# A pair's statistics through ScalarE's queue, the halves of attention's outputs copied and added by VectorE behind the near maximum, and four edits at the ends of the later stages

## The chip, the core and the metric

The kernel is one program on one core of a Trainium2 chip. The metric is the device time of one execution in microseconds (us), the median of several runs. A core has five engines that each take their instructions in order: TensorE (PE), VectorE (DVE), ScalarE (ACT), GpSimd (POOL) and SyncE (SP). They wait for each other by semaphores. DMAs are issued here by SP, POOL and ACT, and an engine that waits for a semaphore holds up whatever stands behind it in its queue, DMA issues among it.

## The reference

One layer of a decoder over 2048 tokens of width 1024, all in float32:

```python
hn = _rmsnorm(h, ln_mix[i])
z = hn @ w_in[i]
...
att = _dilated_attention(q, k, v, slopes).reshape(B, S, ATT_WIDTH)
pool = _multiscale_pool(u, pool_w[i], pool_scale[i])
h = h + jnp.concatenate([att, pool], axis=-1) @ w_out[i]
hn = _rmsnorm(h, ln_ffn[i])
up = _causal_dwconv(hn @ w_up[i], conv_w[i], conv_b[i])
gate, val = jnp.split(up, 2, axis=-1)
h = h + (jax.nn.silu(gate) * val) @ w_down[i]
g = jax.nn.sigmoid(_rmsnorm(h, ln_ple[i]) @ w_ple_gate[i])
h = h + g * (p[i] @ w_ple[i])
...
return _rmsnorm(h, ln_final)
```

The attention has 8 heads of 64 and three branches, with windows of 128, 512 and 2048 tokens and dilations of 1, 4 and 16; only the causal keys within the window count. Each branch gives an output, a row maximum and a softmax denominator, and the branches are mixed with weights denominator x exp(maximum - largest maximum).

## The kernel before

**Stages.** By the profile's time: the input projection and the pooling groups to 403 us, attention to about 738, the output projection with its norms to 905, the up products with convolution and gate (44 turns) to 1805, the down products to 2281, and the per-layer-embedding gate with the final norm, in five pieces of tokens (three of 512, two of 256), to the end. Nearly every float32 product is made of three matmuls on values that are split into a high part (made by ACT) and a low part (what is left, made by DVE or POOL): `split`, L83, and `mm3`, L88.

**Attention** (`phase_attention`). Heads go in pairs. A pair has 32 steps, 16 blocks of 128 queries for each head, and the kernel has 128 steps in all. In a step PE makes near scores (L572, L573) and far scores (L561, L562), DVE adds the biases and takes the row maxima (near L577, far L583), ACT makes the exponentials with their sums (near L589, far L593), PE turns them over (L600), ACT copies the high half (L613), DVE makes the low half (L617), and PE multiplies with the values (L628 far, L642 near). The order on all engines is written by hand: the list `ord` in `CFG` names the stages with a lag in steps, and every step runs down that list.

```python
'ord': [['B', 0], ['M', 0], ['N', 0], ['S', 1], ['o', 7], ['F', 0], ['h', 2], ['nm', 0], ['fm', 0], ['l', 2], ['T', 1], ['V', 6], ['W', 6], ['ne', 0], ['fe', 0]]
```

N and F are the scores, nm and fm the maxima, ne and fe the exponentials, T the turn, h and l the halves, V and W the values, o the fold, S the statistics, M the mixing.

**The fold.** Four query blocks make a group, with one output of 128 x 512 for the far branches and one for the near branch. The upper and lower 64 partitions of the output are the products with the high and low halves of the values, so they are added: `halves_sum` lets ACT copy one half to SBUF (L657) and DVE add the other (L658). That occurs at every second step, 64 times. The output's pool in PSUM has one buffer, so the next V on PE waits for that add.

**The pair's statistics.** At the end of each of the first three pairs, `mix_stats` has PE transpose maxima and denominators (L754, L757), DVE copy them to SBUF (sx L759, sy L761), and POOL's queue store them to memory (std L763, stf L764) and load them in another layout (sn L767, sf L771). With d counted in steps from the next pair's start, `mix_lift` (L845 to L850, DVE and ACT) works on them at d = 9 and `mix_weights` (to L863) at d = 10; from d = 13 POOL fetches the weights (wb, L874), multiplies (L884 to L891) and stores the results (L907, L908) in four rounds, four steps apart, which reach into the next pair.

**Later places.** In `phase_rest` the last turn of the up products writes yg (L1495) to memory from SP's queue (L1496); the down products read it as ra (L1542, also SP) and split it. Before the last stage the gate's weights (wg) and the embedding's (w_ple, raw tile rwp) are loaded and split. `close` makes a piece's result, and `add_square` sums its squares (L155). A list `tk` holds what is due after so many ticks; a tick is a group of gate and embedding matmuls. `one` makes the final norm's sums on PE (st, L100) and its inverse root.

Of the kernel before, what the change touches and what calls it, by code (L numbers as in the profile page):

```python
# [13 lines left out]
ALU = mybir.AluOpType  # L14
# [5 lines left out]
KD = D // P  # L20
S = 2048
# [19 lines left out]
V_N = V_CB + 2 * NF  # L41


CFG = {"tt": 2, "ee": 2, 'ord': [['B', 0], ['M', 0], ['N', 0], ['S', 1], ['o', 7], ['F', 0], ['h', 2], ['nm', 0], ['fm', 0], ['l', 2], ['T', 1], ['V', 6], ['W', 6], ['ne', 0], ['fe', 0]], 'perm': [3, 2, 1, 0], 'fp': [[0], [1], [2], [3]], 'np': [[0, -1], [1], [2], [3]], 'm': [9, 10, 13, 4, 6, 7]}


class Shared:
# [438 lines left out]
def phase_attention(tc, g, mx, near_b, far_b):  # L486
# [5 lines left out]
    with ExitStack() as ctx:  # L492
# [145 lines left out]
        def far_pv(gi, kbs, first):  # L638
            gr = groups[gi]
            for kb in kbs:  # L640
                for pt in (gr.h, gr.l):
# [7 lines left out]
                    )  # L649
                    first = False  # L650

        def halves_sum(dst, o, e):

            mine = slice(DH * e, DH * e + DH)
            other = slice(DH * (1 - e), DH * (1 - e) + DH)
            ev = sb.tile([P, CH], F32, tag="ev", bufs=2, name="ev")
            nc.scalar.copy(ev[mine], o[other])  # L657
            nc.vector.tensor_tensor(dst, o[mine], ev[mine], op=ALU.add)  # L658

        def values(v):  # L660
            gi, part = v // 4, v % 4
# [15 lines left out]
        def fold(v):  # L677
# [9 lines left out]
            else:  # L687
                halves_sum(pt.s1[mine, q * CH : (q + 1) * CH], gr.o, e)
                groups.pop(gi)

        def stats(s):
            if (s + 1) % (2 * NQ) == 0:
                pr = s // (2 * NQ)
                if pr < NPAIR - 1:
                    mix_stats(nc, g, mx, ps_t, pr, pairs[pr])
                else:
                    last_near(nc, g, mx, ps_t, pairs[pr])

        def mix(s):
            for pr in range(NPAIR - 1):  # L700
                d = s - (pr + 1) * 2 * NQ
                if d == CFG["m"][0]:
                    mix_lift(nc, g, mx, pairs[pr])
                if d == CFG["m"][1]:
                    mix_weights(nc, g, mx, pr, pairs[pr])
                for c in range(NCH):
                    if d == CFG["m"][2] + CFG["m"][3] * c:
                        mix_fetch(nc, g, mx, nc.gpsimd, pr, pairs[pr], c)
                    if d == CFG["m"][2] + CFG["m"][3] * c + CFG["m"][4]:
                        mix_products(nc, g, mx, nc.gpsimd, pairs[pr], c)  # L710
                    if d == CFG["m"][2] + CFG["m"][3] * c + CFG["m"][5]:
                        mix_store(nc, g, mx, nc.gpsimd, nc.gpsimd, pr, pairs[pr], c)()
# [5 lines left out]
        with tc.manual_schedule(engines=set(EN.values())):  # L718
            for dst, src in load_qk(0):
                rdma(nc, dst, src)  # L720
            for q in range(4):
                for which in ("v3", "v1"):
                    rdma(nc, *load_v(0, which, q))
            queue = []
            stages = {
                "F": far_scores, "N": near_scores, "fm": far_max, "nm": near_max, "fe": far_exp, "ne": near_exp,
                "T": turn, "h": high, "l": low, "V": values, "W": values_b, "S": stats, "M": mix, "o": fold, "B": begin
            }
            for s in range(NS + 10):
                if s < NS:  # L730
                    h, n = divmod(s, NQ)
                    if n == 1 and h + 1 < H:
                        queue += load_qk(h + 1)
                    if queue:
                        rdma(nc, *queue.pop(0))
                    for pr in range(1, NPAIR):
                        if s - 2 * NQ * (pr - 1) in V_STEPS:
                            rdma(nc, *load_v(pr, *V_STEPS[s - 2 * NQ * (pr - 1)]))
                if s == NS + 2:
                    last_far(nc, g, mx, ps_t, pairs[NPAIR - 1])  # L740
                    pieces = pairs[NPAIR - 1].pieces = last_weights(nc, mx, pairs[NPAIR - 1])
                for nm, lag in CFG["ord"]:
                    if 0 <= s - lag < NS or nm == "M":
                        stages[nm](s - lag)
                for _ in range({NS + 3: 3, NS + 4: 2, NS + 5: 1}.get(s, 0)):
                    next(pieces)
# [4 lines left out]
def mix_stats(nc, g, sb, psum, pr, pt):  # L751

    tp = psum.tile([P, 1024], F32, tag="t", name="tps")
    nc.tensor.transpose(tp[:64, :P], pt.st1.rearrange("p a e n -> p (a e n)"), g.ident)  # L754
    far = tp[:16, CH:].rearrange("p (c r) -> p r c", r=4)
    for r in range(4):
        nc.tensor.transpose(far[:, r, :], pt.st3[:, r].rearrange("p a e i -> p (a e i)"), g.ident)  # L757
    sx = sb.tile([64, P], F32, tag="sx", name="sx")
    nc.vector.tensor_copy(sx, tp[:64, :P])  # L759
    sy = sb.tile([16, CH], F32, tag="sy", name="sy")  # L760
    nc.vector.tensor_copy(sy, tp[:16, CH:])  # L761
    q = nc.gpsimd
    q.dma_start(g.std[pr], sx)  # L763
    q.dma_start(g.stf[pr], sy)  # L764
    pt.sn = sb.tile([P, 2, 2, 16], F32, tag="sn", name="sn")
    pt.sf = sb.tile([P, 2, 2, 16], F32, tag="sf", name="sf")
    q.dma_start(  # L767
        pt.sn.rearrange("p a e r -> p (a e) r"),
        g.std[pr].rearrange("(ae n) q -> ae (n q)", n=NQ).rearrange("ae (i r) -> i ae r", r=16),
    )  # L770
    q.dma_start(  # L771
        pt.sf.rearrange("p a e r -> p (a e) r"),
        g.stf[pr].rearrange("(ae n) q -> ae (n q)", n=4).rearrange("ae (i r) -> i ae r", r=16),
    )
# [138 lines left out]
def phase_rest(tc, g, mxs, mx, last_pair, xT, pT, w_out, w_up, w_down, w_gate, w_ple, outT):  # L913
# [3 lines left out]
    with ExitStack() as ctx:  # L917
# [463 lines left out]
        with tc.manual_schedule(engines=set(EN.values())):  # L1381
# [8 lines left out]
            for i in range(len(turns) + 1):  # L1390
# [102 lines left out]
                    add(cur.uv[:, hi_], cur.c)  # L1493
                if prev:
                    nc.vector.tensor_tensor(prev.yg, prev.yg, prev.yv, op=ALU.mult)  # L1495
                    nc.sync.dma_start(g.act[prev.f][:, prev.half * 1024 : prev.half * 1024 + 1024], prev.yg)  # L1496
                splits(6)
                sum_t4(i + 2)
                after(6)
# [118 lines left out]
        aux[0] = db  # L1618
        ahead(len(order))
        wg = [units.pop(("g", 0, k)) for k in range(NW)]  # L1620
        wg += [load_w2(db, rows(w_gate, k), f"wg{k}", nc.vector if k % 2 else None) for k in range(NW, KD)]
        wp = []
        for k in range(KP):
            raw = sb.tile([P, 1024], F32, tag="raw", bufs=2, name="rwp")
            nc.sync.dma_start(raw, rows(w_ple, k))
            hi = db.tile([P, 1024], F32R, tag="wph", bufs=2, name="wph")
            lo = db.tile([P, 1024], F32R, tag="wpl", bufs=2, name="wpl")
            split(nc, hi, lo, raw, nc.vector if k % 2 else None)
            wp.append((hi, lo))

        HF = CH // 2
# [17 lines left out]
        for i, (t0, n, off, row) in enumerate(pieces):  # L1649
# [23 lines left out]
            def close(j, gp, pl):  # L1673
# [10 lines left out]
                if last and j == KD - 1:  # L1684
                    sq = db.tile([P, CH], F32, tag="nt", bufs=3, name="sq")[:, :n]
                    nc.scalar.activation(sq, ht, AF.Square)
                    sqs.append(sq)
                else:
                    add_square(nc, db, acc, ht, j == 0)

            if i == 0:
                for grp in range(2):
# [43 lines left out]
                for j in range(KD):  # L1736
                    tk.later(j // 2, lambda j=j: scaled(j))

            tk.later(1, one)
        tk.flush()  # L1740


# [127 lines left out]
```

## Time and profile before

| what | us |
|---|---|
| median of 3 runs | 2526.32 (2522.40 to 2528.23) |
| the profiled execution | 2537.44 |
| its span | 2535.3 |
| busy PE, DVE, ACT, POOL | 2417.9, 1579.9, 1106.6, 527.8 |
| attention, 403 to 738: PE, DVE, ACT, POOL busy | 273.8, 245.7, 257.2, 115.5 |
| mean granted clock: whole span, attention | 0.978, 0.93 |

The page sums each engine's busy time over the span; PE is the fullest by far, but attention, with PE busy 273.8 of 335 us, is its loosest long stage. In the views, `out<-in` names tiles, a bracket at the end of a timeline row gives the idle time before an instruction and what ended it, and "PEclk" or "granted clock" is 1.00 at full speed.

### The profile page before, as it was taken

The numbers are of one execution on the slowest core, as the hardware profiler recorded it, in microseconds if no ns is written. First come the engines' busy times: TensorE is split into PE (matmuls) and PEld (weight loads), VectorE is DVE, ScalarE is ACT, GpSimd is POOL, SyncE is SP. The second block draws the span as 40 slices with busy tenths as digits, with TensorE's granted clock in tenths as the row PEclk, the third lists the DMA queues.
The fourth block names the chain that finished last, engine by engine and source line by source line (L and its number), as shares of the span: only waits on it lengthen the run. The fifth ranks groups of instructions, "written<-read, shape, count | busy, mean of one in ns | idle before, by whom it ended". The sixth has DMA issues, their size and how long they took to land.

```text
span 2535.3 us, 31890 instructions
## 1 busy us (share of the span) xinstructions
PE 2417.9 (95%) x11515; PEld 2026.2 (80%) x11515; DVE 1579.9 (62%) x2414; ACT 1106.6 (44%) x1923; POOL 527.8 (21%) x436
## 2 busy tenths in 40 slices
PE   8999998887779999999999999999999999999998
PEld 7888887776667877888887888888788888887788
DVE  6645427876664467888888666666435464444664
ACT  5423326887641135444446444444323243323332
POOL 3312221054420023343340000000122222212000
PEclk9999999998889999999999999999999999999999
DMA  7534358696646774445556333333646474644332
GB/s 238 170 123 179 141 176 252 168 202 169 159 161 224 220 241 168 166 173 184 174 196 207 121 121 133 121 120 109 199 134 218 142 239 143 198 145 143 121 104 88
DMA packets 205933, 424.10 MB, mean 167 GB/s; under 512 B 39392, under 2 KB 65632, under 8 KB 202704
## 3 DMA queue, kind: packets, MB, share of 16 engines
q1 hardware_dynamic: 170720, 368.94, 46.1%
q0 software_dynamic: 18912, 25.75, 3.1%
q10 hardware_dynamic: 16144, 27.38, 2.9%
q8 instruction: 91, 1.49, 0.3%
q14 instruction: 66, 0.54, 0.1%
HBM read 290.01 MB, written 131.89 MB: 166 GB/s over the span
## 4 chain that ended last, share of the span: by engine, by line
PE 74%; DMA 8%; issue 7%; DVE 4%; ACT 2%; POOL 2%; SPq 0%; POOLq 0%; DVEq 0%; ACTq 0%
PE ua L1298 18%; PE uc L1298 9%; PE dn L89 6%; PE dn L90 6%; PE dn L91 6%; PE ub L1298 4%; PE z L91 4%; PE z L89 4%; PE z L90 4%; DMA wb<-wd 3%; PE o L91 2%; PE o L89 2%; PE o L90 2%; PE gp L89 2%; PE gp L90 2%
## 5 line engine op out<-in xcount | busy, mean ns | idle before, releaser
L89 PE MATMUL dn<-ah,hd 128*128 128x512 f32 x704 | 275.4, 391 | 4.5 <-ACT ah L84 4.5
L90 PE MATMUL dn<-al,hd 128*128 128x512 f32 x704 | 275.0, 391 | 0.1
L91 PE MATMUL dn<-ah,ld 128*128 128x512 f32 x704 | 274.7, 390 | 0.0
L85 POOL TENSOR_TENSOR ld<-rd,hd 128x1024 fp32r<-128x1024 f32 x42 | 100.9, 2403 | 814.9 <-DVE yg L1318 466.3
L84 ACT CAST hd<-rd 128x1024 fp32r<-128x1024 f32 x88 | 92.6, 1052 | 265.9 <-PE dn L90 230.4
L85 DVE TENSOR_TENSOR al<-ra,ah 128x512 fp32r<-128x512 f32 x88 | 116.4, 1325 | 136.3 <-ACT ah L84 136.3
L89 PE MATMUL z<-hnh,wh 128*128 128x512 f32 (+1 forms) x480 | 171.2, 357 | 9.1 <-ACT hnh L252 5.8
L90 PE MATMUL z<-hnl,wh 128*128 128x512 f32 (+1 forms) x480 | 171.0, 356 | 2.5 <-DVE hnl L253 2.4
L91 PE MATMUL z<-hnh,wl 128*128 128x512 f32 (+1 forms) x480 | 170.7, 356 | 2.3 <-POOL wl L85 1.7
L89 PEld LDWEIGHTS dn<-ah,hd 128*128 128x128 f32 x704 | 132.7, 189 | 32.2 <-ACT ah L84 4.9
L90 PEld LDWEIGHTS dn<-al,hd 128*128 128x128 f32 x704 | 132.7, 188 | 28.1 <-DVE al L85 0.6
L91 PEld LDWEIGHTS dn<-ah,ld 128*128 128x128 f32 x704 | 132.7, 189 | 27.9
L85 DVE TENSOR_TENSOR wu<-ru,wu 128x1024 fp32r<-128x1024 f32 x88 | 127.5, 1448 | 0.0
L155 DVE TENSOR_TENSOR acc<-acc,sq 128x512 f32<-128x512 f32 (+1 forms) x125 | 91.2, 729 | 50.9 <-ACT sq L154 37.7
L1298 PE MATMUL uc<-a22h,wu 128*128 128x512 f32 x352 | 116.8, 393 | 1.8 <-DVE uv L1321 1.8
L1298 PE MATMUL ub<-a12h,wu 128*128 128x512 f32 x352 | 116.8, 393 | 0.6 <-ACT a12h L1354 0.6
L1298 PE MATMUL ua<-s2h,wu 128*128 128x512 f32 x352 | 115.7, 389 | 0.7 <-ACT ug L1435 0.7
L1298 PE MATMUL ua<-s1h,wu 128*128 128x512 f32 x352 | 115.7, 390 | 0.0
L1298 PE MATMUL uc<-s3h,wu 128*128 128x512 f32 x352 | 115.7, 389 | 0.0
L1298 PE MATMUL ua<-s4h,wu 128*128 128x512 f32 x352 | 115.5, 389 | 0.0
L1298 PE MATMUL ua<-a11h,wu 128*128 128x512 f32 x352 | 115.5, 389 | 0.0
L85 DVE TENSOR_TENSOR ld<-rd,hd 128x1024 fp32r<-128x1024 f32 x46 | 56.7, 1233 | 90.4 <-ACT hd L84 90.4
(322 smaller groups left out, 6486.1 us busy)
## 6 DMA issues: line engine op xcount, KB each, us to landing
rd<-in_w_down_dram SPq DMA_DIRECT2D x88, 512.0 KB, 3.6
ru<-in_w_up_dram SPq DMA_DIRECT2D x66, 512.0 KB, 4.1
act<-yg SPq DMA_DIRECT2D x44, 512.0 KB, 3.2
ra<-act SPq DMA_DIRECT2D x88, 256.0 KB, 3.8
wr<-in_w_in_dram SPq DMA_DIRECT2D x64, 256.0 KB, 4.0
nt<-h SPq DMA_DIRECT2D x56, 256.0 KB, 3.8
h<-h SPq DMA_DIRECT2D x56, 256.0 KB, 5.4
td<-t SPq DMA_DIRECT2D x22, 512.0 KB, 2.6
```

Of the source, the lines that this page charges most:

```text
L84: nc.scalar.copy(hi, src)
L85: (low or nc.gpsimd).tensor_tensor(lo, src, fp(hi), op=ALU.subtract)
L89: nc.tensor.matmul(ps, wh, ah, start=first, stop=False)
L90: nc.tensor.matmul(ps, wh, al, start=False, stop=False)
L91: nc.tensor.matmul(ps, wl, ah, start=False, stop=last)
L155: nc.vector.tensor_tensor(acc[:, :n], acc[:, :n], sq[:, :n], op=ALU.add)
L1298: nc.tensor.matmul(pst, x[:, ksl], y, start=first and k == 0 and n == 0, stop=k == HK - 1 and n == 2, skip_group_check=True)
```

## The change

There are six edits, and a change that goes with the second (the seventh).

1. The fold's copy moves from ACT to DVE, and copy and add are no longer issued in stage o: they are put off (`due`) to a new stage p, which stands behind nm in the list.
2. The statistics' DMAs move from POOL's queue to ACT's. The stores come at d = 1 (L780, L781 of the changed kernel), the loads at d = 4 (L788, L792).
3. The last yg is stored from POOL's queue in place of SP's.
4. The low halves of the gate's later weights and of w_ple are all made by DVE (before, by POOL and DVE in turn).
5. The squares of the final norm (sq) have two buffers.
6. The final norm's sums (`one`) come one tick later, but for the last piece.
7. `mix_stats` keeps sx and sy for the later calls.

```diff
--- before.py
+++ after.py
@@ -41,7 +41,7 @@
 V_N = V_CB + 2 * NF
 
 
-CFG = {"tt": 2, "ee": 2, 'ord': [['B', 0], ['M', 0], ['N', 0], ['S', 1], ['o', 7], ['F', 0], ['h', 2], ['nm', 0], ['fm', 0], ['l', 2], ['T', 1], ['V', 6], ['W', 6], ['ne', 0], ['fe', 0]], 'perm': [3, 2, 1, 0], 'fp': [[0], [1], [2], [3]], 'np': [[0, -1], [1], [2], [3]], 'm': [9, 10, 13, 4, 6, 7]}
+CFG = {"tt": 2, "ee": 2, 'ord': [['B', 0], ['M', 0], ['N', 0], ['S', 1], ['o', 7], ['F', 0], ['h', 2], ['nm', 0], ['p', 7], ['fm', 0], ['l', 2], ['T', 1], ['V', 6], ['W', 6], ['ne', 0], ['fe', 0]], 'perm': [3, 2, 1, 0], 'fp': [[0], [1], [2], [3]], 'np': [[0, -1], [1], [2], [3]], 'm': [9, 10, 13, 4, 6, 7]}
 
 
 class Shared:
@@ -649,13 +649,19 @@
                     )
                     first = False
 
+        due = []
+
         def halves_sum(dst, o, e):
 
             mine = slice(DH * e, DH * e + DH)
             other = slice(DH * (1 - e), DH * (1 - e) + DH)
             ev = sb.tile([P, CH], F32, tag="ev", bufs=2, name="ev")
-            nc.scalar.copy(ev[mine], o[other])
-            nc.vector.tensor_tensor(dst, o[mine], ev[mine], op=ALU.add)
+
+            def both():
+                nc.vector.tensor_copy(ev[mine], o[other])
+                nc.vector.tensor_tensor(dst, o[mine], ev[mine], op=ALU.add)
+
+            due.append(both)
 
         def values(v):
             gi, part = v // 4, v % 4
@@ -688,6 +694,10 @@
                 halves_sum(pt.s1[mine, q * CH : (q + 1) * CH], gr.o, e)
                 groups.pop(gi)
 
+        def folded(v):
+            while due:
+                due.pop(0)()
+
         def stats(s):
             if (s + 1) % (2 * NQ) == 0:
                 pr = s // (2 * NQ)
@@ -699,6 +709,10 @@
         def mix(s):
             for pr in range(NPAIR - 1):
                 d = s - (pr + 1) * 2 * NQ
+                if d == 1:
+                    mix_stats_store(nc, g, pr, pairs[pr])
+                if d == 4:
+                    mix_stats_load(nc, g, mx, pr, pairs[pr])
                 if d == CFG["m"][0]:
                     mix_lift(nc, g, mx, pairs[pr])
                 if d == CFG["m"][1]:
@@ -724,7 +738,7 @@
             queue = []
             stages = {
                 "F": far_scores, "N": near_scores, "fm": far_max, "nm": near_max, "fe": far_exp, "ne": near_exp,
-                "T": turn, "h": high, "l": low, "V": values, "W": values_b, "S": stats, "M": mix, "o": fold, "B": begin
+                "T": turn, "h": high, "l": low, "V": values, "W": values_b, "S": stats, "M": mix, "o": fold, "p": folded, "B": begin
             }
             for s in range(NS + 10):
                 if s < NS:
@@ -759,9 +773,16 @@
     nc.vector.tensor_copy(sx, tp[:64, :P])
     sy = sb.tile([16, CH], F32, tag="sy", name="sy")
     nc.vector.tensor_copy(sy, tp[:16, CH:])
-    q = nc.gpsimd
-    q.dma_start(g.std[pr], sx)
-    q.dma_start(g.stf[pr], sy)
+    pt.sx, pt.sy = sx, sy
+
+
+def mix_stats_store(nc, g, pr, pt):
+    nc.scalar.dma_start(g.std[pr], pt.sx)
+    nc.scalar.dma_start(g.stf[pr], pt.sy)
+
+
+def mix_stats_load(nc, g, sb, pr, pt):
+    q = nc.scalar
     pt.sn = sb.tile([P, 2, 2, 16], F32, tag="sn", name="sn")
     pt.sf = sb.tile([P, 2, 2, 16], F32, tag="sf", name="sf")
     q.dma_start(
@@ -1493,7 +1514,7 @@
                     add(cur.uv[:, hi_], cur.c)
                 if prev:
                     nc.vector.tensor_tensor(prev.yg, prev.yg, prev.yv, op=ALU.mult)
-                    nc.sync.dma_start(g.act[prev.f][:, prev.half * 1024 : prev.half * 1024 + 1024], prev.yg)
+                    (nc.gpsimd if over else nc.sync).dma_start(g.act[prev.f][:, prev.half * 1024 : prev.half * 1024 + 1024], prev.yg)
                 splits(6)
                 sum_t4(i + 2)
                 after(6)
@@ -1618,14 +1639,14 @@
         aux[0] = db
         ahead(len(order))
         wg = [units.pop(("g", 0, k)) for k in range(NW)]
-        wg += [load_w2(db, rows(w_gate, k), f"wg{k}", nc.vector if k % 2 else None) for k in range(NW, KD)]
+        wg += [load_w2(db, rows(w_gate, k), f"wg{k}", nc.vector) for k in range(NW, KD)]
         wp = []
         for k in range(KP):
             raw = sb.tile([P, 1024], F32, tag="raw", bufs=2, name="rwp")
             nc.sync.dma_start(raw, rows(w_ple, k))
             hi = db.tile([P, 1024], F32R, tag="wph", bufs=2, name="wph")
             lo = db.tile([P, 1024], F32R, tag="wpl", bufs=2, name="wpl")
-            split(nc, hi, lo, raw, nc.vector if k % 2 else None)
+            split(nc, hi, lo, raw, nc.vector)
             wp.append((hi, lo))
 
         HF = CH // 2
@@ -1686,7 +1707,7 @@
                     nc.scalar.activation(sq, ht, AF.Square)
                     sqs.append(sq)
                 else:
-                    add_square(nc, db, acc, ht, j == 0)
+                    add_square(nc, db, acc, ht, j == 0, 2)
 
             if i == 0:
                 for grp in range(2):
@@ -1736,7 +1757,7 @@
                 for j in range(KD):
                     tk.later(j // 2, lambda j=j: scaled(j))
 
-            tk.later(1, one)
+            tk.later(1 if last else 2, one)
         tk.flush()
 
 
```

On VectorE, in the first pair, around one fold: ev is the copied half, s the sum, L577 the near and L583 the far maximum, L617 a low half of the turned exponentials.

```order
 L617 TENSOR_TENSOR ptl<-tp,pth 128x640
-L658 TENSOR_TENSOR s_3827<-o,ev 64x512
 L577 ISA tt,st_3824<-sn,nb_3798 128x256
 L577 ISA st_3824 128x1
+L661 COPY ev<-o 64x512
+L662 TENSOR_TENSOR s_3827<-o,ev 64x512
 L583 ISA tt,st_3825<-sf,fb_3799 128x512
 L583 ISA st_3825 128x1
```

The add has moved behind the near maximum and the copy has come in ahead of it, both before the far maximum.

On ScalarE, at the start of the second pair: L613 is a high half, L589 and L593 are the exponentials, std and stf the stored statistics.

```order
 L589 ACTIVATE ee,st_3824<-tt,st_3824 128x256
 L593 ACTIVATE ee,st_3825<-tt,st_3825 128x128
-L657 COPY ev<-o 64x512
 L613 CAST pth<-tp 128x512
 L589 ACTIVATE ee,st_4624<-tt,st_4624 128x256
 L593 ACTIVATE ee,st_4625<-tt,st_4625 128x512
+L780 DMA std_115<-sx 64x128
+L781 DMA stf_119<-sy 16x512
 L613 CAST pth<-tp 128x384
```

The copy of each fold is gone, and the two stores stand behind the exponentials of the pair's first step. The loads stand three steps further on, behind the exponentials of the fourth:

```order
 L589 ACTIVATE ee,st_4624<-tt,st_4624 128x128
 L593 ACTIVATE ee,st_4625<-tt,st_4625 128x128
-L657 COPY ev<-o 64x512
+L788 DMA sn<-std_115 128x4x16
+L792 DMA sf<-stf_119 128x4x16
 L613 CAST pth<-tp 128x512
```

Each load reads what a store has written, so ACT stands at it until that store has landed.

## The prediction

> **What bounds the kernel now.** I read the page first, then the windows of the attention stretch (403 to about 738 us), its waits, single source lines and the timeline of one fold. The page gives the span of the profiled execution; its time is 2537.44 us, so 2.1 us lie around the span, and the median of the runs shown, 2526.32, is 11.1 below it. I make the sum against the profiled execution and take the same difference off the median. The windows have busy time and count for PE, PEld, DVE, ACT and POOL, then the granted clock, the DMA share and GB/s.
>
> ```profile
> span 2535.3 us, 31890 instructions
> 441.90:558.00 116.10, 103.57 (x652) 91.00 (x651) 94.14 (x289) 99.41 (x277) 32.54 (x35) 1.00 0.77 183
> 570.00:575.00 5.00, 0.00 (x0) 0.00 (x0) 0.00 (x0) 0.00 (x0) 0.00 (x0) 0.72 0.97 278
> 575.00:580.00 5.00, 0.00 (x0) 0.00 (x0) 0.00 (x0) 0.00 (x0) 1.60 (x2) 0.50 0.66 217
> ```
>
> In the running attention no engine is full: of 116.1 us PE works 103.6, ACT 99.4, DVE 94.1. They pass work round in a ring. From 570 to 580, though, PE, VectorE and ScalarE do nothing, POOL works 1.6 us, and DMAs run. The waits of 560 to 590, and one of 650 to 675, name the cause (total, times, longest):
>
> ```profile
> DVE lo L845 <- DMA sf<-stf: 12.1, 1, 12.1
> PE sn L572 <- DVE st L577: 11.6, 1, 11.6
> POOL sn L767 <- DMA std<-sx: 10.9, 1, 10.9
> DVE lo L845 <- DMA sf<-stf: 11.9, 1, 11.9
> ```
>
> VectorE's lift of the pair's statistics waits 12 us for their load, and everything queued behind it waits too. The statistics were ready long before:
>
> ```profile
> L759 DVE COPY sx<-tps x3: 283/283/283, 473.5 to 633.5; 64x128 f32<-64x128 f32 x3
> L763 POOL DMA_DIRECT2D std<-sx x3: 556/556/558, 474.1 to 648.7; - x3
> DMA to landing us min/median/max: 3.2/6.4/12.9
> ```
>
> For the third pair, sx was copied at 633.5, but POOL, which issues in order and still had the pair before to fetch and multiply, came to std only at 648.7. It then stood until std had landed before it issued the load. Of the six stores and loads through std, the median landing is 6.4 us.
>
> **The statistics through ScalarE.** One step is half a fold cycle. The lines of the fold's add (first and last start) give the cycles:
>
> ```profile
> L658 DVE TENSOR_TENSOR s<-o,ev x3: 683/683/683, 492.6 to 501.9; 64x512 f32<-64x512 f32 x3
> L658 DVE TENSOR_TENSOR s<-o,ev x3: 682/682/683, 566.2 to 588.4; 64x512 f32<-64x512 f32 x3
> L658 DVE TENSOR_TENSOR s<-o,ev x3: 682/683/683, 652.7 to 675.4; 64x512 f32<-64x512 f32 x3
> L658 DVE TENSOR_TENSOR s<-o,ev x10: 683/683/695, 675.4 to 715.8; 64x512 f32<-64x512 f32 x10
> ```
>
> The same two cycles around the lift take 9.3 us in the first pair, which didn't stall, but 22.2 and 22.7 in the two that did. If the stalls go, 12.9 + 13.4 = **26.3 us** are saved; the 24.0 of the two waits are in this, and the rest is PE at half clock behind them. Will they go? The stores now go out one step behind the boundary and the loads three steps later, 3 x 2.25 = 6.8 us at the cycle of 40.4 / 9 = 4.49 us that the last row gives, and 7.4 at the longer cycle below; the median landing of 6.4 fits in. From load to lift there are five steps, 11 to 12 us, so a median landing hides again. ACT's queue has none of POOL's fetches ahead of it. The new wait is ACT's own, at the load: behind it on ACT are the exponentials and high halves, and PE's transposes wait for those. At the worst landing, 12.9, it is 5.5 us a pair, 16.5 in all; at the median nothing. I take 0.2 a pair, as the landings lie nearer to the median: **+0.6**. Four DMA issues of about 0.56 us a pair, by L763's row, go on ACT, which has 17 of the 116 us free before and more after.
>
> **The fold.** ScalarE's copy leaves, and the two halves of the fold become one chain on VectorE behind the near maximum. What it was:
>
> ```profile
> L657 ACT COPY ev<-o x64: 577/582/587, 416.1 to 735.4; 64x512 f32<-64x512 f32 x64
>   ACT ev L657: 52.3, 56
> ```
>
> So 64 copies, 37 us of ACT, go, and with them 52.3 us that VectorE stood waiting for them in 56 places. In return DVE gets 64 copies. Taken by busy time that is a gain. But the output has one buffer, so PE's next values (V) wait for the add, and what matters is the ring through it. Timeline of one fold (start, duration, what, idle before it and its releaser):
>
> ```profile
> 697.58 0.68 DVE L658 TENSOR_TENSOR s<-o,ev 64x512 f32<-64x512 f32 x1 [1.11 <-ACT ev L657]
> 698.19 0.41 DVE L577 CUSTOM_DVE_ANT_0 tt<-sn,nb 128x256 f32<-128x256 f32 x1
> 698.32 0.50 PE L642 MATMUL o<-pth,v 128*128 128x512 f32 x1 [0.30 <-DVE s L658]
> 698.53 0.07 DVE L577 DVE_READ_ACCUMULATOR2_ANT st<- 128x1 f32 x1
> 701.01 0.28 PE L573 MATMUL sn<-ks,qll 128*128 128x256 f32 x1
> ...
> 693.80 0.39 PE L628 MATMUL o<-pth,v 128*128 128x256 f32 x1 [0.44 <-DVE s L658]
> 696.71 0.28 PE L573 MATMUL sn<-ks,qll 128*128 128x256 f32 x1
> ```
>
> Before, V waits a few tenths for an add that itself waits for ACT, and the near maximum (L577) comes behind the add. After, the add comes behind the near maximum, which waits for PE's near scores of the same step. The ring is then: add, V, PE's matmuls of two steps as far as the second near scores, near maximum, copy, add. Add to V is 698.32 - 697.58 = 0.74 us. V to the second L573 is 2.69 in this fold and 2.91 in the one before it. In the longer one the transposes partly wait for VectorE's low halves, which have more room after, so I take 2.75. Two more steps:
>
> ```profile
> 585.95 0.28 PE L573 MATMUL sn<-ks,qll 128*128 128x256 f32 x1
> 586.27 0.42 DVE L577 CUSTOM_DVE_ANT_0 tt<-sn,nb 128x256 f32<-128x256 f32 x1 [0.59 <-PE sn L573]
> L761 DVE COPY sy<-tps x3: 669/669/669, 473.7 to 633.8; 16x512 f32<-16x512 f32 x3
> ```
>
> L573 to a near maximum that waits for it is 0.32. VectorE's copy of 512 from PSUM has its row in sy, 0.67; with the 0.04 by which L577 stood behind L573's end, copy to add is 0.71. Near maximum to copy is 0.34 when the copy may overlap it (as its accumulator read starts at 698.53) and 0.41 when it may not. Which holds is told by these, a fold of the other head of the pair:
>
> ```profile
> 706.61 0.69 DVE L658 TENSOR_TENSOR s<-o,ev 64x512 f32<-64x512 f32 x1 [1.06 <-ACT ev L657]
> 707.34 0.42 DVE L577 CUSTOM_DVE_ANT_0 tt<-sn,nb 128x256 f32<-128x256 f32 x1
> ```
>
> Here, where the add works on the upper 64 partitions and L577 begins at the lowest, L577 starts 0.73 behind it; in the first head, both at the lowest, 0.61. The new copy always crosses from one half of the partitions to the other, so I take 0.41. The Trainium skill ("VectorE: DVE Perf Modes", section "Two Vector instructions with no wait between them") says that a VectorE instruction whose operands start in another group of 32 partitions than those before is held until they have finished; the two gaps above agree with it. Without that rule the sum would be 54 x 0.07 = 3.8 us less.
>
> The cycle comes to 0.74 + 2.75 + 0.32 + 0.41 + 0.71 = **4.93 us**, against 4.49 to 4.50 before: +0.43. Of the 63 cycles some 54 are such (the others are at the start, the end and the three boundaries), so **+23.2 us**. By the shorter steps (2.69, 0.34) it is 4.80, +16; with 2.91 it is 5.09, +32. At the three boundaries sx and sy (0.28 + 0.67) stand in the same ring: between 0 and 0.95 each, I take 0.8, as nothing beside them shortens: **+2.4**. At attention's end the last folds are serial, up to the copy's 0.67: **+0.6**. The far maximum now stands 1.4 us later, but its exponentials are needed by the transposes a step on, behind V; ACT has the copy's 0.58 less.
>
> Attention: -26.3 + 0.6 + 23.2 + 2.4 + 0.6 = **+0.5 us**.
>
> **The end of the up products.** The store of the last yg leaves SP's queue (timeline):
>
> ```profile
> 1798.16 4.37 SPq L1527 DMA_DIRECT2D rd<-in_w_down_dram  x2
> 1803.28 0.33 SPq L1496 DMA_DIRECT2D act<-yg  x1
> 1809.19 0.80 PE L89 MATMUL dn<-ah,hd 128*128 128x512 f32 x1 [4.48 <-ACT ah L84]
> ```
>
> SP stood on that store until 1803.28, and ra, the input that PE misses for 4.48 us, was issued behind it at 1803.66. Without it ra follows the rd loads, which end at 1802.53: **-1.1 us**. POOL pays an issue beside other work.
>
> **The low halves of the PLE weights**, now all on VectorE:
>
> ```profile
> 2296.83 2.37 POOL L85 TENSOR_TENSOR lwg<-rwg,hwg 128x1024 fp32r<-128x1024 f32 x1 [5.09 <-ACT hwg L84]
> 2293.41 1.21 DVE L85 TENSOR_TENSOR lwg<-rwg,hwg 128x1024 fp32r<-128x1024 f32 x1
> 2309.82 0.80 PE L89 MATMUL pl<-pph,wph 128*128 128x512 f32 x1 [2.60 <-ACT wph L84]
> ```
>
> PE waits 2.60 us for wph, whose raw load needs a buffer that these subtractions free: 1.21 on DVE for 2.37 on POOL. At most 1.2 is gained, nothing if the load is late for itself; I take **-0.9**. The second buffer for sq has no wait to remove: 0.
>
> **The final norm's st, a tick later:**
>
> ```profile
> 2356.30 1.05 PE L100 MATMUL st<-ones,acc 128*128 128x1 f32 x8 [2.76 <-DVE acc L155]
> 2357.00:2361.00 4.00, 4.00 (x14) 3.18 (x14) 2.18 (x7) 0.89 (x2) 1.01 (x1) 0.57 0.00 0
> ```
>
> PE waits 2.76 us for the sum of squares and then runs 4 us at a clock of 0.57, 1.7 us lost. A tick later, with a group of gate matmuls between, both go: **-4.4**. The later pieces' rows show no such wait, and the end is held by the last piece, whose order stays.
>
> Sum: 0.5 - 1.1 - 0.9 - 4.4 = -5.9, so 2531.5 for a profiled execution and **2520.4** for the median; by the fold's ends 2513 to 2529.
>
> **The rivals.** (1) PE's chain does not shrink: the longer 2.91, in all cycles, gives 5.09 and +8.6 more, 2529; 2534 with ACT's wait at its bound of 5.5 in one pair. 0.20, since half of the folds show it now. (2) The fold costs no time: no engine is full in the row of 441.9, ACT loses a seventh of its work, and if the cycle stays at 4.50 the 26 us disappear as well, 2526.3 - 5.9 - 25.6 = 2495. Against it stands the ring: the near maximum can't start before its scores. 0.18, as two tenths hidden in PE's part would carry half of it. (3) The stall stays: std or stf land as at the worst, or SP's loads, on whose landing the ACT queue may also wait, hold the load back; each of the two stalls comes back once store and load together take over 19 us (8 steps), 2520.4 + 24.0 = 2544. 0.06; the median pair needs 13. (4) The clock falls. PE's idle time before V grows from 0.4 to about 1 us a cycle, and these show what a gap can do:
>
> ```profile
> 720.00:725.00 5.00, 3.54 (x20) 2.92 (x19) 3.22 (x5) 1.27 (x3) 0.00 (x0) 0.73 0.02 3
> 722.21 0.55 PE L600 MATMUL tp<-ident,ee 128*128 128x128 f32 x2 [1.46 <-DVE nr L789]
> ```
>
> A gap of 1.46 us was followed by half clock. From about that size this decides; if it strikes in one cycle of three, 18 x 1.7 = 31 us, 2551. 0.06, as the gaps stay under it. The Trainium skill ("TensorE: Matmul & The Clock Gate", "Part 1: The HAM clock gate") has the clock halve only after an idle window of about 3.4 us; by it this rival would cost nothing, but the 1.46 us gap here does not agree.
>
> **How the numbers follow.** The forecast has 0.50. What a measurement tells from no change is 0.2%, 5.05 us: 2521.3 to 2531.4. The forecast's ends put half of it below that, half within; rival 1 is half within and half above; 2 is below; 3 and 4 above. Faster 0.25 + 0.18 = 0.43; same 0.25 + 0.10 = 0.35; slower 0.10 + 0.12 = 0.22. The range leaves out 3 and 4 (0.12) and the lower part of 2 (0.08): 2497 to 2538. The forecast's own is 2513 to 2529.
>
> **What would show it.** No wait of L845 on sf and no idle stretch near 570 and 657; adds 4.8 to 5.1 us apart, V waiting about 1 us for them; no wait of 2.76 at the first st; ra issued at the end of the rd loads. It is wrong if the adds stay 4.5 apart, if the clock in attention is below 1, or if L845 still waits.

## The result, and the profile after

The changed kernel takes 2545.09 us in the median (2542.78 to 2547.17, 4 runs), the kernel before 2527.28 (2522.40 to 2528.93, 4 runs). The ratio is 1.0067 with a 95% interval of 1.0047 to 1.0087: slower by 17.8 us, where 5.9 us faster was forecast. The profiled executions lie much nearer to each other, 2542.78 against 2537.44, and that difference of 5.3 us has to be explained apart from the 17.8.

The windows of a plain stretch of its attention and of the first st (busy time and count of PE, PEld, DVE, ACT and POOL, then the clock, the DMA share and GB/s):

```profile
598.00:642.00 44.00, 34.16 (x226) 31.42 (x226) 39.19 (x105) 29.34 (x86) 24.80 (x25) 1.00 0.72 170
2362.80:2377.80 15.00, 15.00 (x71) 12.45 (x71) 6.25 (x14) 3.84 (x8) 1.01 (x1) 1.00 0.06 18
```

DVE is now the busiest engine of this stretch, 39.2 of 44 us, and PE works 34.2; before, PE worked 103.6 of 116.1. The clock is 1.00 here in spite of PE's gaps, but not in all of attention: behind each lift of the statistics it falls to half, as this window behind the first lift shows.

```profile
506.00:512.50 6.50, 5.73 (x22) 5.29 (x23) 4.16 (x12) 3.04 (x9) 2.94 (x4) 0.50 0.19 30
```

At the first st PE no longer stops. The line of the fold's add in after, with first and last start, over the whole span and over a plain stretch:

```profile
L662 DVE TENSOR_TENSOR s<-o,ev x64: 682/689/695, 415.1 to 750.7; 64x512 f32<-64x512 f32 x64
L662 DVE TENSOR_TENSOR s<-o,ev x9: 682/683/695, 599.7 to 639.5; 64x512 f32<-64x512 f32 x9
```

The same line in a second execution of before (run 1 below):

```profile
L658 DVE TENSOR_TENSOR s<-o,ev x64: 682/689/696, 413.9 to 730.2; 64x512 f32<-64x512 f32 x64
```

From first to last add, after takes 335.6 us, before 316.3 here and 321.6 in its first profile (416.7 to 738.3, L658 x64). A plain cycle is 39.8 / 8 = 4.98 us. One ring, as the timeline of after has it:

```profile
522.71 0.68 DVE L662 TENSOR_TENSOR s<-o,ev 64x512 f32<-64x512 f32 x1
523.49 0.35 PE L628 MATMUL o<-pth,v 128*128 128x256 f32 x1 [1.11 <-issue]
526.28 0.28 PE L573 MATMUL sn<-ks,qll 128*128 128x256 f32 x1
526.60 0.42 DVE L577 CUSTOM_DVE_ANT_0 tt<-sn,nb 128x256 f32<-128x256 f32 x1 [0.32 <-PE sn L573]
527.06 0.69 DVE L661 COPY ev<-o 64x512 f32<-64x512 f32 x1
527.79 0.68 DVE L662 TENSOR_TENSOR s<-o,ev 64x512 f32<-64x512 f32 x1
```

Add to V 0.78, V to the second near scores 2.79, to the near maximum 0.32, to the copy 0.46, to the add 0.73: 5.08 us, link by link the ring of the prediction. PE stands 1.11 us before V; the bracket names no releaser, but V starts 0.10 us after the add has ended (522.71 + 0.68).

The waits of after between 403 and 745 us have these left of the statistics (total, times, longest):

```profile
ACT pth L613 <- DMA stf<-sy: 4.5, 2, 2.4
DVE lo L866 <- DMA sf<-stf: 4.3, 2, 3.1
```

The two waits of 12 us are gone; ACT and the lift now wait a few us each.

### The profile page after: what moved, and what is told of

It is laid out like the page before. It is cut to its first block, busy times and chain, and to the rows that moved or that the text cites. A ratio compares the mean times of both kernels' runs of the same rounds, so it can differ in the third digit from the quotient of the medians.

```text
span 2540.8 us, 31872 instructions
## 1 busy us (share of the span) xinstructions
PE 2406.5 (95%) x11515; PEld 2023.3 (80%) x11515; DVE 1637.3 (64%) x2480; ACT 1070.3 (42%) x1859; POOL 513.5 (20%) x423
## 4 chain that ended last, share of the span: by engine, by line
PE 80%; DMA 6%; DVE 5%; issue 4%; ACT 1%; POOL 0%; SPq 0%; POOLq 0%; DVEq 0%; ACTq 0%
PE ua L1319 18%; PE uc L1319 9%; PE dn L91 6%; PE dn L90 6%; PE dn L89 6%; PE ub L1319 4%; PE z L89 4%; PE z L91 4%; PE z L90 4%; PE o L91 2%; PE o L89 2%; PE o L90 2%; PE gp L89 2%; PE gp L91 2%; PE gp L90 2%
```

## The experiments

Ratios are against runs of the kernel before in the same job.

**1. The kernel before once more.** No edit.

> The kernel before, profiled once more. Profile against profile the changed kernel is only 5.3 us slower (2542.8 against 2537.4), but in the medians it is 17.8 us slower, so one of the two profiled executions is not typical. Theory S (the stalls vary): before's first profile had unusually long stalls at the second and third pair's lift (12.1 and 11.9 us); another execution has less, together 8 to 16 us, and is 2522 to 2530 us long. Theory R (the ring alone): the two waits are again 12 us each and the difference lies elsewhere.

It took 2524.83 us. Of its waits in all of attention:

```profile
DVE lo L845 <- DMA sf<-stf: 17.7, 2, 11.0
```

The two stalls make 17.7 us, not 24.0: 11.0 and 6.7. Theory S expected 8 to 16 us of stalls, 1.7 too few, and 2522 to 2530 us for the execution, which holds. The 19 runs of before in this job lie between 2516.97 and 2535.32, around 2526.73, so the execution on which the prediction was built, 2537.44, was 10.7 us above that median. From first to last add it was 5.3 us longer than this one; the remainder lies outside that stretch.

**2. The fold alone.**

```diff
-            nc.scalar.copy(ev[mine], o[other])
-            nc.vector.tensor_tensor(dst, o[mine], ev[mine], op=ALU.add)
+            def both():
+                nc.vector.tensor_copy(ev[mine], o[other])
+                nc.vector.tensor_tensor(dst, o[mine], ev[mine], op=ALU.add)
+            due.append(both)
...
+ ['p', 7] behind ['nm', 0]
```

> Before with edit 1 alone: the fold on VectorE behind the near maximum, the statistics still through POOL. Theory R (the ring through near scores, near maximum, copy, add and values sets the cycle): adds 4.9 to 5.1 us apart, +28 us from the cycles, minus what POOL's queue catches up on in the longer steps, which shortens the two stalls: 2540 to 2556. Rival (the moved fold costs nothing by itself, and the loss comes from ScalarE's queue): 2520 to 2528.

2546.47 us, ratio 1.0074 [1.0054, 1.0094], within the 2540 to 2556 of theory R: the fold alone is as slow as the whole change. Lines of its adds, of sx and of std:

```profile
L662 DVE TENSOR_TENSOR s<-o,ev x64: 682/688/695, 415.3 to 747.7; 64x512 f32<-64x512 f32 x64
L662 DVE TENSOR_TENSOR s<-o,ev x9: 682/683/695, 596.5 to 636.2; 64x512 f32<-64x512 f32 x9
L769 DVE COPY sx<-tps x3: 283/283/283, 479.5 to 645.8; 64x128 f32<-64x128 f32 x3
L773 POOL DMA_DIRECT2D std<-sx x3: 553/553/556, 480.1 to 646.6; - x3
```

The cycle is 39.7 / 8 = 4.96 us. And the stalls are gone, although the statistics go through POOL as ever: the third std is issued 0.8 us behind its sx (646.6, 645.8), not 15.1 as in the first profile. The waits of this execution have none of the lift on sf. This is what the prediction had not seen: a pair that takes longer gives POOL the time to end its rounds, and the stall goes without edit 2. At the second pair the times can be taken apart. From the first sx to the second, run 2 takes 83.1 us and the first profile 73.6; from the first sx to the second std, which comes behind POOL's rounds, 84.0 and 91.7. So of the 17.2 us by which that std comes sooner behind its sx, 9.5 are the longer pair, and 7.7 are POOL's own: in its second to fourth round it stands 23.1 us for fetched weights (wb) in the first profile, and 12.4 before the issue of a fetch in run 2. Why it stands less was not tried.

**3. The statistics through ScalarE alone.**

```diff
-    q = nc.gpsimd
-    q.dma_start(g.std[pr], sx)
-    q.dma_start(g.stf[pr], sy)
...
+                if d == 1:
+                    mix_stats_store(nc, g, pr, pairs[pr])
+                if d == 4:
+                    mix_stats_load(nc, g, mx, pr, pairs[pr])
```

> Before with edit 2 alone: the statistics through ScalarE's queue, the fold as before. If the stalls are typically 24 us, as the first profile shows: 2500 to 2505. Theory S: 2510 to 2518. Rival (ScalarE's queue takes on waits of its own that eat the gain): 2522 or more, with waits of several us on ScalarE at the two loads.

2527.53 us, ratio 1.0017 [1.0000, 1.0034]: no gain, as the rival said. The lift waits no more, but ACT's copies do; of the waits in all of attention:

```profile
ACT ev L659 <- DMA v<-vf: 10.3, 2, 5.2
ACT ev L659 <- DMA stf<-sy: 1.8, 1, 1.8
```

ACT's timeline at the second pair's load:

```profile
558.57 0.19 ACT L593 ACTIVATION_READ_ACCUMULATOR ee<-tt,st 128x1 f32 x1
561.45 0.37 ACTq L784 DMA_DIRECT2D sn<-std  x1
563.46 0.37 ACTq L788 DMA_DIRECT2D sf<-stf  x1
563.87 0.58 ACT L659 COPY ev<-o 64x512 f32<-64x512 f32 x1 [5.11 <-DMA v<-vf]
```

The stores of that pair, issued at 551.65 and 552.16, and a load of v on SP's queue, issued at 547.85, with the time to landing as the last number:

```profile
std<-sx ACTq DMA_DIRECT2D x1, 32.0 KB, 9.8
stf<-sy ACTq DMA_DIRECT2D x1, 32.0 KB, 10.8
v<-vf SPq DMA_DIRECT2D x1, 512.0 KB, 15.6
```

ACT is ready at 558.8 and issues the first load at 561.45, just when std has landed (551.65 + 9.8), and the second at 563.46; the fold's copy behind them waits 5.11 us, and the add and V behind that. The second load was held past stf's own landing (552.16 + 10.8 = 562.96), until SP's load of v had landed (547.85 + 15.6 = 563.45), and it is that load which the bracket names. At the third pair it is the same, 627.85 + 15.6 = 643.45 against an issue at 643.54, so the prediction's remark under rival 3, that ACT's queue may also wait for SP's loads, holds here; why it does was not tried. In the profile attention is 313.0 us from first to last add (414.6 to 727.6): 3.3 less than in the second profile of before. The lift's 17.7 us of stalls are gone, but ACT waits 12.1 us at its loads in their place, and PE's clock falls to half there as well.

**4. The later stages alone** (edits 3 to 6 of the diff).

> Before with edits 3 to 6 alone (yg's store, low halves on VectorE, two buffers for sq, st a tick later). In the two profiles the stretch from the first gate matmul to the end is 7 us shorter after, and the change from up to down products is no shorter: 2517 to 2522. Rival (that stretch differs by chance): 2525 to 2529.

2519.44 us, ratio 0.9965 [0.9952, 0.9979]: 7.3 us faster, within the 2517 to 2522 expected. PE's waits at the first st and at the embedding in before's second execution:

```profile
PE st L100 <- DVE acc L155: 2.4, 1, 2.4
PE pl L91 <- POOL wpl L85: 1.5, 1, 1.5
```

and here:

```profile
PE pl L89 <- ACT wph L84: 1.1, 1, 1.1
PE pl L91 <- DVE wpl L85: 0.8, 2, 0.5
```

The wait at st is gone, those for the low halves are smaller. All of PE's waits for the gate's and the embedding's weights together are 5.3 us in the first profile of before, 3.9 in the second and 2.4 here.

**5. The changed kernel without edit 2** (statistics through POOL again).

> The changed kernel without edit 2: fold on VectorE behind the near maximum and the edits 3 to 6, the statistics through POOL's queue again. Theory C (the longer cycles by themselves give POOL the time to store the statistics at once, so edit 2 has nothing left to save, and its loads through ScalarE's queue land later): faster than the changed kernel, 2536 to 2541, the cycles around the lift about 5.8 and 6.0 us, no wait of the lift. Rival (edit 2 is needed beside the fold): 2550 or more, with a wait of the lift on sf.

2538.11 us, ratio 1.0044 [1.0028, 1.0061], within the 2536 to 2541 of theory C. The changed kernel had 1.0067 [1.0047, 1.0087]. By the medians edit 2 costs some 6 or 7 us beside the fold, though these two intervals overlap. The traces show where: around the lifts. At the second lift (three adds, two cycles), in after:

```profile
L662 DVE TENSOR_TENSOR s<-o,ev x3: 682/682/683, 584.4 to 599.7; 64x512 f32<-64x512 f32 x3
sf<-stf ACTq DMA_DIRECT2D x1, 32.0 KB, 14.8
```

and in run 5:

```profile
L662 DVE TENSOR_TENSOR s<-o,ev x3: 682/683/684, 588.6 to 600.3; 64x512 f32<-64x512 f32 x3
```

15.3 us against 11.7. In after that is where the lift waits 3.1 us for sf, whose load was issued at 574.54 and landed 14.8 us later. Over the three lifts these pairs of cycles take 41.2 us in after, 35.6 in run 5 and 35.6 in run 2.

**6. The copy on VectorE, but copy and add at the old place**, with the later stages' edits:

```diff
-            nc.scalar.copy(ev[mine], o[other])
+            nc.vector.tensor_copy(ev[mine], o[other])
```

> Edits 3 to 6, and the fold's copy on VectorE but copy and add at the old place, ahead of the near maximum. Theory R (what costs is the place behind the near maximum, as a ring with the near scores): adds 4.3 to 4.6 us apart, 2505 to 2525, the rest decided by POOL's stalls, which grow as the cycle shrinks. Rival E (what costs is VectorE's work, a copy of 0.67 us at every second step): adds 4.9 or more apart, 2535 to 2545.

2520.48 us, ratio 0.9967 [0.9950, 0.9984], the same as without it (run 4). Its adds:

```profile
L658 DVE TENSOR_TENSOR s<-o,ev x8: 682/690/695, 599.0 to 630.2; 64x512 f32<-64x512 f32 x8
```

and its wait at the lift, of the whole attention:

```profile
DVE lo L845 <- DMA sf<-stf: 17.0, 2, 12.0
```

31.2 / 7 = 4.46 us a cycle: theory R stands against E. VectorE's copy, 0.69 us in this run, costs no time that shows; its place behind the near maximum does. With cycles this short the stalls are there again, 17.0 us.

**7. Both behind the near maximum, but the copy on ScalarE** (`nc.scalar.copy` in `both`), with the later stages' edits:

> Edits 3 to 6, and copy and add behind the near maximum, but the copy on ScalarE (behind the high half in its queue). Theory R: without the serial copy of 0.71 us the ring is 0.74 + 2.75 + 0.32 + 0.4 = 4.2 us and no longer decides; adds 4.3 to 4.7 us apart, 2510 to 2528. Rival (the place alone costs, whoever copies): 4.9 or more, 2535 to 2545.

2525.38 us, ratio 0.9994 [0.9977, 1.0011]. Here neither side was right as a whole: the cycle is the rival's (4.89 for its 4.9 or more), the time is theory R's (2510 to 2528), 10 us below the rival's. The adds of a plain stretch:

```profile
L662 DVE TENSOR_TENSOR s<-o,ev x9: 682/683/695, 581.5 to 620.6; 64x512 f32<-64x512 f32 x9
```

and the timeline from one add to the next:

```profile
521.39 0.68 DVE L662 TENSOR_TENSOR s<-o,ev 64x512 f32<-64x512 f32 x1 [0.84 <-ACT ev L661]
522.45 0.51 ACT L593 ACTIVATE ee<-tt,st 128x256 f32<-128x256 f32 x1 [0.59 <-DVE st L583]
525.22 0.58 ACT L661 COPY ev<-o 64x512 f32<-64x512 f32 x1
525.84 0.68 DVE L662 TENSOR_TENSOR s<-o,ev 64x512 f32<-64x512 f32 x1 [0.35 <-ACT ev L661]
```

39.1 / 8 = 4.89 us a cycle; the one shown, 4.45, is the shortest of its pair. The far maximum waits behind the add, ACT waits 0.59 us for the far maximum, and the next copy stands at the end of ACT's queue, behind two rounds of exponentials and high halves. It is another ring from add to add, through ScalarE. So whoever copies, an add between the near and the far maximum costs 0.4 to 0.5 us in a plain cycle. Over a whole pair who copies still matters. The second pair's adds, which no stall touches in these three, in before, in run 2 and here:

```profile
L658 DVE TENSOR_TENSOR s<-o,ev x17: 682/683/695, 492.6 to 566.2; 64x512 f32<-64x512 f32 x17
L662 DVE TENSOR_TENSOR s<-o,ev x17: 682/683/695, 501.5 to 584.6; 64x512 f32<-64x512 f32 x17
L662 DVE TENSOR_TENSOR s<-o,ev x17: 682/684/696, 496.1 to 575.9; 64x512 f32<-64x512 f32 x17
```

73.6, 83.1 and 79.8 us: the late place costs 6.2 us a pair with the copy on ScalarE and 9.5 with the copy on VectorE. The run supports theory C in part: with these longer cycles the lift waited once, 7.3 us, not twice, although the statistics went through POOL.

**8. The changed kernel without the fold** (edit 1 undone).

> The changed kernel without edit 1: statistics through ScalarE's queue and the edits 3 to 6, the fold as before. From the two parts by themselves (+0.8 and -7.3 us in the medians): 2518 to 2522. Rival (the parts help each other): 2512 or less.

2520.67 us, ratio 0.9976 [0.9958, 0.9994]: within the 2518 to 2522 of the sum of the parts, and only the later stages' edits are worth something.

**9 to 11. The loads three steps later**, so that the stores have landed:

```diff
-                if d == 4:
+                if d == 7:
                     mix_stats_load(nc, g, mx, pr, pairs[pr])
-'m': [9, 10, 13, 4, 6, 7]
+'m': [13, 14, 16, 3, 6, 7]
```

> The changed kernel with the fold as before (edit 1 undone), the loads of the statistics three steps later (d = 7), the lift and weights at 13 and 14, and POOL's rounds from d = 16 every three steps. Theory W (what ate the gain of edit 2 beside the old fold are ScalarE's waits at its loads, 5 to 7 us a pair, since the stores land 10 us after their issue): no wait at the loads, none at the lift, cycles of 4.2 to 5.6 throughout, about 20 us less than with the loads at d = 4: 2498 to 2506. Rival (the time goes elsewhere, to POOL's rounds, which now end nearer to attention's end, or to the DMAs): 2512 or more.

> The same with the fold's copy on VectorE ahead of the near maximum. Theory W: adds 4.4 to 4.55 us apart, no stall and no wait at the loads, within 4 us of the run with the old fold: 2496 to 2508. Rival as there: 2512 or more.

> The changed kernel with loads, lift and rounds at the later steps, the fold left behind the near maximum. Theory R and C: the cycles stay at 4.87 to 5.1 us, the waits at load and lift (some 6 us in all) go: 2536 to 2541, as with the statistics through POOL. Rival (the lift's timing is what made the changed kernel slow): 2525 or less.

They took 2536.99 (1.0034 [1.0013, 1.0054]), 2542.89 (1.0054 [1.0034, 1.0073]) and 2549.43 us (1.0078 [1.0053, 1.0103]): all slower than before. Theory W's numbers fell, and run 11 missed the 2536 to 2541 expected of it, as well as its rival's 2525 or less. **12. A middle course:** loads at d = 6, lift and weights at 11 and 12, rounds as before.

> The changed kernel with the fold as before (edit 1 undone), loads at d = 6, lift and weights at 11 and 12, POOL's rounds where they were (from 13, every four steps). In the run with all of that three steps later, ScalarE's waits at its loads were gone but POOL's later rounds held up the folds for 16 us a pair. Theory W2 (both waits can be left out at once): cycles of 4.2 to 5.7 throughout, 2502 to 2512, against 2520.7 with the loads at d = 4. Rival (POOL has no room at all for a later start): a wait of the folds on POOL's products and 2520 or more.

2524.57 us, ratio 0.9992 [0.9980, 1.0004]; the rival was right. Of the waits of run 9:

```profile
DVE s L660 <- POOL m L902: 31.5, 2, 16.0
```

and of run 12:

```profile
DVE s L660 <- POOL m L902: 15.7, 2, 9.1
```

In run 9 ACT waits no more at its loads, in run 12 once, 4.9 us, but in both the adds wait for POOL's products (m), which still read the sums of an earlier pair. As far as these runs show, then, POOL's rounds have no room to start later in a pair of the old length: each of these orders only chose who waits. Run 11 keeps the slow fold, and its adds wait 7.1 us for POOL once; the timing of the lift isn't what made the changed kernel slow.

The best versions are runs 4, 6 and 8, at 2519 to 2521 us; none beats run 4, edits 3 to 6 alone.

## Why the prediction was wrong

**Where the difference lies.** The forecast was 2520.4 us and the measurement 2545.09, 24.7 more. Of these, 11.3 are in the profiled execution, forecast at 2531.5 and measured at 2542.78. The other 13.4 are in the step from that execution to the median.

**The fold.** The ring and each of its links were right. The plain cycle measured 4.98 for 4.93, 54 x 0.05 = 2.7 us more. The step that failed is that the cycles around a lift were counted as ordinary ones. The two cycles there, in run 2:

```profile
L662 DVE TENSOR_TENSOR s<-o,ev x3: 682/683/683, 584.6 to 596.5; 64x512 f32<-64x512 f32 x3
```

They take 11.9 us against the 9.4 of the pair of before that did not stall, and over the three lifts 7.5 us more than there, for the 2.6 of six ordinary cycles. Two things make this, both put at nothing in the sum. Taken against the same places of the first pair, which has no lift, the lift's own cycle grew by 0.5 us more, and the cycle behind it by 1.1 to 1.3 us more.

On VectorE, the lift's three instructions (0.4 us) and those of the weights (L867 to L872) come ahead of a near maximum:

```profile
588.10 0.18 DVE L867 TENSOR_TENSOR dn<-wts,sn 128x32 f32<-128x32 f32 x1
589.17 0.42 DVE L577 CUSTOM_DVE_ANT_0 tt<-sn,nb 128x256 f32<-128x256 f32 x1
```

That is 1.1 us for the weights, and copy and add stand behind this near maximum, so that work is in the ring, as the prediction had only seen for sx and sy. And the clock falls behind the lift. PE's V behind that add, and the windows ahead of it and from it on:

```profile
591.13 0.76 PE L642 MATMUL o<-pth,v 128*128 128x512 f32 x1 [1.89 <-issue]
587.60:591.00 3.40, 1.65 (x13) 1.35 (x11) 3.23 (x13) 2.33 (x7) 0.76 (x1) 0.99 0.67 236
591.10:594.10 3.00, 2.96 (x11) 2.80 (x12) 1.81 (x8) 1.32 (x4) 1.32 (x2) 0.50 0.06 10
```

PE stood 1.89 us, was busy 1.65 of 3.4 us, and then ran at half clock, so that V to the second near scores took 3.84 us (591.13 to 594.97) where the ring of after, shown above, has 2.79. The same fall comes behind each of the three lifts in run 2, in run 5 and in after. In all, run 2's 332.4 us from first to last add stand against 321.6 - 26.3 = 295.3 for the first profile without its stalls: the fold cost 37.1 us, not 23.2 + 2.4 + 0.6 = 26.2. The 3 us that the plain cycles and the lifts leave of this are in the first pair, at folds that wait for loads and vary between all runs (its first 16 cycles take 83.8 us in after, 86.2 in run 2 and 88.0 in run 5).

**"If the stalls go, 26.3 us are saved. Will they go?"** They went, and against the first profile the 26.3 us came off as forecast. But the longer cycles alone remove them (run 2), so edit 2 had nothing to save beside edit 1, and nothing beside the old fold either (run 3). The terms were taken as independent, while the stall was in good part what POOL lacked in a pair's time and the fold made the pair longer. That decides what edit 2 is worth; it does not change the sum. What the sum had too small in this step is the new wait, ACT's at the load, priced at 0.6 us in all by the median landing of 6.4. That median mixes three stores with three loads. The stores of sx alone landed after 6.1 us in the first profile and then, for the second and third pair, after

```profile
std<-sx POOLq DMA_DIRECT2D x1, 32.0 KB, 11.7
std<-sx POOLq DMA_DIRECT2D x1, 32.0 KB, 12.9
```

Two of the three are beyond the 7.4 us after which the load follows. By the prediction's own reckoning, landing less 7.4, they cost 4.3 + 5.5 = 9.8 us. Measured were 4.5 in after and 12.1 in run 3, whose steps are shorter. The lift's 4.3 us in after were not in the sum either. Against the first profile, attention is 37.1 - 26.3 + 3.2 = 14.0 us longer, where +0.5 was forecast. The 3.2 are the difference between after (335.6) and run 2 (332.4): 5.5 more around the lifts, 2.4 less in the first pair.

**"I take the same difference off the median."** This step failed by 13.4 us. The profiled execution of before was 11 us above its median, that of after is 2.3 below its own. Part of those 11 us was in the longer stalls themselves (24.0, in the second profile 17.7), which the change takes away: they can't be taken off again afterwards. Where the rest of the 11 us came from stays open. Profile against profile, +14.0 in attention, some -6.5 in the last stage and -2 elsewhere make the +5.3; the rest of the 17.8 is this step.

**The later stages.** -6.4 was forecast and -7.3 measured (run 4). At st, the wait is gone and the clock is full, as forecast. The low halves gave more than 0.9: PE's waits for these weights shrank by 1.5 to 2.9 us (run 4). The store of yg gave a few tenths at most: ra was issued at the end of the rd loads, as forecast (timeline of SP in after),

```profile
1809.85 4.52 SPq L1548 DMA_DIRECT2D rd<-in_w_down_dram  x2
1814.46 0.86 SPq L1563 DMA_DIRECT2D ra<-act  x2
```

but the waits of PE at this place are these:

```profile
PE dn L89 <- ACT ah L84: 3.3, 1, 3.3
PE dn L90 <- DVE al L85: 1.5, 1, 1.5
```

It waited 3.3 us for the high half and then 1.5 for the low one: 4.8, and 4.6 in run 4, in place of 4.5 and 5.2 in the two profiles of before.

**The rivals.** The fold that costs no time (0.18) is refuted; PE's chain that doesn't shrink (0.20) had the right sign for the ring, 5.09 forecast for all cycles and 4.98 measured. The stall that stays did not occur in after; its cause, slow landings, took a few us. The clock that falls (0.06) was priced at one cycle in three. It came, but behind the lifts and where the ring waits longer (the first pair's loads, the third boundary), not in plain cycles. In plain cycles PE's gap of 1.11 us before V repeats every 5 us at a clock of 1.00; behind each lift of run 2, run 5 and after the clock was at half for 3.4 us or more. Over all of attention it is 0.95 in after and 0.93 in the first profile of before, where it also falls behind the stalls. The Trainium skill ("TensorE: Matmul & The Clock Gate", "Part 1: The HAM clock gate") has the clock halve after an idle window of about 3.4 us. The rows of run 2 do not bear this out: there it halved after 3.4 us in which PE was busy for 1.65. What moved the result most, the cycles around the lifts and the step to the median, was priced by no rival.

## What to carry to other kernels

When one part of a change lengthens a cycle and another removes a wait inside that cycle, the wait has to be priced again at the new length: here a wait that came from an engine with too little time per pair went by itself (run 2), and moving the transfer off that engine then gained nothing. Where an instruction is put in order behind one that waits for another engine, draw the ring from itself to itself and add its links: that gave 4.93 for 4.98, where the busy times said that nothing was full. Then ask which other instructions stand in that queue in some of the cycles, as the lift did here, and what PE's longer gap does to the clock there. When a wait hangs on one kind of transfer, take the landing of that kind alone: the stores took 6.1 to 12.9 us, while the median of stores and loads was 6.4. And take a second profile of the kernel before, or at least ask how far the first lies from the median and in which wait, before a stall that depends on DMA landings is booked as a saving.

## What the hardware showed that was not expected

A 32 KB store to memory landed 9.8 and 10.8 us after its issue from ScalarE's queue in run 3, and the six DMAs through std in after took between 4.2 and 13.6.

PE's clock halved behind 3.4 us in which PE still worked 1.65 us, with a gap of 1.89 (run 2), and stayed full where PE worked 34.2 of 44 us with gaps of 1.11 (after).

ACT's issue of a 32 KB load stood until a 512 KB load on SP's queue had landed, at two places of run 3 (563.46 behind 563.45, 643.54 behind 643.45) and one of run 8 (565.42 behind 565.41).

Executions of one and the same kernel differed by 18 us and more (2516.97 to 2535.32 in 19 runs of before; 2517.26 to 2542.31 in 21 beside runs 9 to 11). The four of the changed kernel lay within 4.4, but the ten of run 5, which had no stall at its lift in the profile, spread over 9.7 and the ten of run 4 over 10.2, so that the stalls make the spread is not shown.
